# Routed experts: the second products' biases as one product with the masked gates

## The chip, the cores and the metric

One core of a Trainium2 chip. The metric is the time of one execution of the program on the device, in microseconds. The kernel before was timed in three runs: median 3362.38 us (3360.96 to 3362.39). The profiled execution took 3356.17 us by the same clock, and its span, from the first to the last recorded instruction, is 3354.4 us.

## What is computed

Two transformer blocks on 512 tokens of width 1024, one after the other, in float32. The change touches the last layer of the second block, a routed mixture of 32 experts: each token takes its four best experts, and their gates are the softmax of four router values. Cut to what matters:

```python
logits = (hf @ w_router + b_router).astype(jnp.float32)
top_val, top_idx = lax.top_k(logits, TOP_K)
gates = jax.nn.softmax(top_val, axis=-1)
...
def expert_block(args):
    e, tok, g = args
    xb = hf[tok]
    gu = xb @ w1[e] + b1[e]
    gate = jnp.minimum(gu[:, :D_FF], SWIGLU_LIMIT)
    up = jnp.clip(gu[:, D_FF:], -SWIGLU_LIMIT, SWIGLU_LIMIT)
    act = (up + 1.0) * gate * jax.nn.sigmoid(SWIGLU_ALPHA * gate)
    return (act @ w2[e] + b2[e]) * g[:, None]
...
out = jnp.zeros((n_tok, d), h.dtype).at[row_tok].add(y.reshape(n_rows, d))
```

`w1` is 1024 x 2048 per expert, `w2` 1024 x 1024, so each expert's weights are 12.6 MB. A token's row of the result is the sum over its experts of the gate times (`act @ w2[e] + b2[e]`); the part with the biases is, for all tokens at once, the matrix of the gates (512 x 32, zero where a token does not take an expert) times `b2` (32 x 1024).

## The kernel before, in words

A float32 product is made of three products of operands split into a high and a low part in the format fp32r: high x high, high x low, low x high (L1377 to L1379). For the weights ScalarE makes the high part (`wh`, L163) and VectorE, or for every twelfth piece GpSimd, the low part (`wl`, L164).

The experts run one after the other (`moe`, L1305 on). A block of 128 rows holds an expert's tokens; a loop at the end, for experts with more than 128 tokens, is not entered with these inputs. The weights come in pieces of 512 KB (256 input rows, 512 output columns), 24 per expert, into 17 raw buffers (`wr`) from SyncE's queue; a raw buffer is free again when its low part is made. `Feed` keeps up to five split pieces ahead of TensorE.

Per expert there are six products with 512 output columns: two for the gate half (`gate`), two for the up half (`up`), two for the second matrix (`outp`). Each (`product`, L1367) is 24 matmuls of 128 x 128 by 128 x 512 into one PSUM bank, and ahead of them one more (L1369) that puts the bias there: a column of `selr`, one-hot for the expert, times the tile `bias`, which holds the biases of all experts in rows 0 to 31 (high) and 32 to 63 (low). Four banks serve the products.

The gate half goes from PSUM through VectorE (`mg`, L1400), ScalarE (sigmoid `ms`, L1402) and VectorE (L1403); the up half through VectorE (`ms` L1409, `mact` L1410). `back` transposes `mact` on TensorE and splits it (`mah`, `mal`), `turn` does the same for the next expert's gathered rows `xf` (`mxh`, `mxl`), after ScalarE has scaled them (`scale`, L1388). `outp` evicts its two products on ScalarE into `my` (L1419), scaled by each row's gate. `my` is 128 x 1024 and has one buffer. `store` (L1422) is an indirect DMA from GpSimd's queue that adds the rows of `my` to the rows of `acc` in device memory; `begin` gathers rows of `hfd` in the same way (L1351).

Each engine works through its instructions in the order in which this code issues them. In iteration `e` of the main loop that is:

```python
n = begin(e + 1) if e + 1 < NE else None
b.up(0)
if prev:
    prev.store()
...
if n:
    n.scale()
b.gate(1, lambda: self.tokens(e + 2, g3(e + 2)) if e + 2 < NE else None)
```

and then `up(1)` with `back(0)` and the next expert's `turn` in its middle, the next expert's `gate(0)` with `back(1)` in its middle, and `outp`. `prev.store()` stands after `up(0)` of the next expert. `gates2` (L1229) runs once, after the first expert's `turn`: it normalises the gates (`gdn`, L1240) and cuts them into three bfloat16 parts (`g3`).

Of the kernel before, what the change touches and what calls it, by code (L numbers as in the profile page):

```python
# [7 lines left out]
F32 = mybir.dt.float32  # L8
F32R = mybir.dt.float32r
BF = mybir.dt.bfloat16  # L10
I32 = mybir.dt.int32
U32 = mybir.dt.uint32
AF = mybir.ActivationFunctionType
ALU = mybir.AluOpType
# [33 lines left out]
def layout(inp):  # L48
    f = lambda n: np.asarray(inp[n])
    pk = lambda w: w.reshape(-1, 128, w.shape[-1]).swapaxes(0, 1)  # L50
    chunk = lambda w, c: np.stack([pk(w[:, i:i + c]) for i in range(0, w.shape[1], c)])
    o = {}
    o["xT"] = pk(f("x")[0].T)
    o["pT"] = pk(f("p")[0, 0].T)
    o["memT"] = pk(f("mem_2")[0].T)
    o["w_in"] = chunk(f("w_in")[0][:, :1920], 128)
    o["w_in_v"] = pk(f("w_in")[0][:, 1920:])
    o["w_out"] = chunk(f("w_out")[0], 128)
    o["w_q"] = chunk(f("w_q")[0], 128)
    o["sk"] = f("sub_keys")[0].reshape(16, 128, 128).transpose(2, 0, 1)  # L60
    o["u_t"] = f("expert_u")[0].reshape(128, 128, 8, 128).transpose(0, 3, 2, 1)
    o["u_r"] = f("expert_u")[0]
    o["v_r"] = f("expert_v")[0]
    o["w_pe"] = chunk(f("w_pe")[0], 128)
    o["w_pg"] = chunk(f("w_pg")[0], 128)
    o["w_in_2"] = chunk(f("w_in_2")[0], 128)
    o["w_out_2"] = np.stack([chunk(f("w_out_2")[0][:512], 128), chunk(f("w_out_2")[0][512:], 128)])
    o["w_mem_q"] = chunk(f("w_mem_q_2")[0], 128)
    wide = lambda w: np.stack([np.stack([pk(w)[:, i:i + 2, j:j + 512] for i in range(0, 8, 2)]) for j in range(0, w.shape[1], 512)])
    o["w_mem_k"] = chunk(f("w_mem_kv_2")[0][:, :1024], 128)  # L70
    o["w_mem_v"] = wide(f("w_mem_kv_2")[0][:, 1024:])
    o["w_in_2v"] = wide(f("w_in_2")[0][:, 1024:1536])[0]
    o["w_mem_o"] = chunk(f("w_mem_o_2")[0], 128)
    o["w_pool"] = f("w_pool_2")[0].transpose(1, 0, 2)
    o["w_s"] = f("w_s")[0].transpose(2, 0, 1)
    o["w_router"] = pk(f("w_router_2")[0])
    o["w1"] = f("w_expert_in_2")[0].reshape(NE, 8 // CK, CK, 128, 4, 512).transpose(0, 4, 1, 3, 2, 5)
    o["w2"] = f("w_expert_out_2")[0].reshape(NE, 8 // CK, CK, 128, 2, 512).transpose(0, 4, 1, 3, 2, 5)
    b = np.concatenate([f("b_expert_in_2")[0], f("b_expert_out_2")[0]], 1)
    o["b12"] = np.concatenate([b, b, np.zeros((64, 3072), np.float32)], 0)  # L80
    cols = []
    for n in COLS:
        a = f(n)
        a = a.reshape(-1) if a.ndim == 1 else a[0]
        if n in ("conv_a_w", "conv_b_w"):
            cols.append(a.reshape(a.shape[0], -1, 128).transpose(2, 1, 0).reshape(128, -1))
        else:
            cols.append(a.reshape(-1, 128).T)
    o["cols"] = np.concatenate(cols, 1)
    row = lambda a: np.broadcast_to(a.reshape(1, -1), (128, a.size))  # L90
    o["rows"] = np.concatenate([row(f("ln_c_g")[0]), row(f("ln_c_b")[0]), row(f("b_router_2")[0]),
                                row(f("g_final_2")), row(f("g_ffn_2")[0])], 1)
    bs = f("b_s")[0].reshape(3, 2, 1, 128)
    o["b_s"] = np.broadcast_to(bs, (3, 2, 64, 128)).reshape(3, 128, 128).transpose(1, 0, 2)
    i = np.arange(128)
    one = np.float32(1)
    mats = [np.eye(128, dtype=np.float32), np.broadcast_to(i.astype(np.float32), (128, 128)),
            (i[:, None] < i[None, :]) * one, (i[:, None] >= i[None, :]) * one,
            (i[:, None] // 64 == i[None, :] // 64) * np.float32(1 / 64), np.ones((128, 128), np.float32)]
    sel = np.zeros((128, 128), np.float32)  # L100
    sel[:64, :32] = (i[:64, None] % 32 == i[None, :32])
    sel[:, 32] = i
    w = 2 ** (np.arange(4) + 1)
    t = np.arange(16)
    cnt = one / np.minimum(t[None, :] + 1, w[:, None]).astype(np.float32)
    sel[:, 64:128] = cnt.reshape(1, 64)
    mats.append(sel)
    o["consts"] = np.concatenate(mats, 1)
    return {k: np.ascontiguousarray(v) for k, v in o.items()}
# [37 lines left out]
class Body:  # L147
# [1085 lines left out]
    def gates2(self):  # L1233

        nc, cp, ge = self.nc, self.cp, self.ge
        sm = cp.tile([128, 4], F32, name="smm")
        nc.vector.tensor_reduce(sm, ge[:, :, 32:36], axis=AX.X, op=ALU.add)
        nc.vector.reciprocal(sm, sm)
        g = cp.tile([128, 4, 32], F32, name="gdn")
        nc.vector.tensor_tensor(g, ge[:, :, 0:32], sm.rearrange("p (t o) -> p t o", o=1).to_broadcast([128, 4, 32]), op=ALU.mult)  # L1240
        self.g3 = g3 = cp.tile([128, 4, 3, 32], BF, name="g3")
        for k in range(3):
            nc.vector.tensor_copy(g3[:, :, k], g)
            if k < 2:
                nc.vector.tensor_sub(g, g, g3[:, :, k])
# [59 lines left out]
    def moe(self):  # L1305
        tc, nc, A = self.tc, self.nc, self.A
        acc = self.acc
        hfd = self.hfd
        with ExitStack() as st:
            pool = lambda **k: st.enter_context(tc.tile_pool(bufs=1, **k))  # L1310
            xp = pool(name="xx")
            wst = st.enter_context(ExitStack())
            wp = wst.enter_context(tc.tile_pool(name="xw", bufs=1))
            rp = wst.enter_context(tc.tile_pool(name="xr", bufs=1))
# [1 line left out]
            bias = self.bias  # L1316
# [49 lines left out]

            def product(src, feed, sel, boff, mid=None):  # L1367
                ps = self.bank()
                nc.tensor.matmul(ps, sel.to_broadcast([128, 128]), bias[:, boff:boff + 512], start=True, stop=False)  # L1369
                for kk in range(8 // CK):  # L1370
                    if mid and kk == 4 // CK:
                        mid()
                    wh, wl = feed.take()
                    for k in range(CK):
                        i = CK * kk + k
                        a = src[0][:, i]
                        nc.tensor.matmul(ps, a, wh[:, k], start=False, stop=False)  # L1377
                        nc.tensor.matmul(ps, a, wl[:, k], start=False, stop=False)
                        nc.tensor.matmul(ps, src[1][:, i], wh[:, k], start=False, stop=(i == 7))  # L1379
                return ps  # L1380

            class Block:
# [32 lines left out]
                def outp(b, mid=None):  # L1415
                    b.y = y = xp.tile([128, 1024], F32, name="my", bufs=1)
                    for c in range(2):
                        ps = product(b.as_, b.feed, b.sel, 2048 + 512 * c, None if c else mid)
                        nc.scalar.activation(y[:, 512 * c:512 * c + 512], ps, AF.Copy, scale=b.f[:, 1:2])  # L1419

                def store(b):
                    nc.gpsimd.indirect_dma_start(out=acc, out_offset=bass.IndirectOffsetOnAxis(ap=b.ix, axis=0), in_=b.y,  # L1422
                                                 in_offset=None, bounds_check=511, oob_is_err=False, compute_op=ALU.add)

            def begin(e):
                return Block(xf, *self.xidx.pop(e), self.selr[:, e:e + 1], feed)
            g3 = lambda e: self.g3[:, :, :, e]
            b = begin(0)
# [14 lines left out]
            for e in range(NE):  # L1443
                n = begin(e + 1) if e + 1 < NE else None
                b.up(0)
                if prev:
                    prev.store()
                if e + 2 < NE:
                    self.places(e + 2)
                if e == 1:  # L1450
                    self.blocks()
# [4 lines that stand above are left out]
                def turns():  # L1456
                    b.back(0)
                    if n:
                        n.turn()
                b.up(1, turns)  # L1460
                if n:
                    n.gate(0, lambda: b.back(1))
                    b.outp()
                else:
                    b.outp(lambda: b.back(1))
                prev, b = b, n
# [5 lines left out]
            with tc.For_i(0, n, 1) as i:  # L1472
                j = nc.values_load(lst[0:1, bass.ds(i, 1)], engines=[mybir.EngineType.SP, mybir.EngineType.DVE],
                                   min_val=0, max_val=95)
                e = j % 32
# [14 lines left out]
                b = Block(xf, *self.xidx.pop("o"), s2, f2)  # L1490
# [12 lines left out]
            o = []  # L1503
# [39 lines left out]
```

## Time and profile before

| | before |
|---|---|
| median of 3 runs | 3362.38 us |
| profiled execution | 3356.17 us, span 3354.4 us |
| TensorE (PE) busy | 3139.9 us, 94% of the span |
| VectorE (DVE) busy | 2679.3 us, 80% |
| ScalarE (ACT) busy | 1756.8 us, 52% |
| GpSimd (POOL) busy | 1014.4 us, 30% |
| granted TensorE clock, mean | 0.974 |
| DMA | 819.30 MB, mean 244 GB/s |

The shares are means over stages of different kinds. The experts fill the span from about 2076 us to 3321 us, 1245 us for 32 experts. In the tables below, PE is TensorE's matmuls, PEld its weight loads, DVE VectorE, ACT ScalarE, POOL GpSimd and SP SyncE; times are in microseconds from the start of the span. The recorded end of a matmul is modelled and overlaps the next one, so of matmuls one reads the starts. In rows of the trace `L...` is a line of the kernel, `out<-in` are the program's names of tiles, and the brackets at the end hold the idle time of the engine before the instruction and what ended it.

### The profile page before, as it was taken

The page shows a single profiled execution, that of the slowest core. Times are in us where ns is not written, and L with a number is a line of the kernel's source. Part 1 is how long each engine was busy: PE and PEld are TensorE (multiplying, and loading weights), DVE is VectorE, ACT ScalarE, POOL GpSimd, SP SyncE. Part 2 cuts the span into 40 slices and gives each one's busy share as a digit, 9 for nine tenths or more (in the row PEclk, how much of TensorE's full clock was granted, in tenths as well). Part 3 has the DMA queues.
Part 4 walks back from the last instruction along what each step waited for, and adds up shares of the span by engine and source line. Part 5 has one row for each costly group of instructions (what it writes and reads, how often), then busy time and mean ns, then how long its engine had stood idle before and what let it go on. Part 6 is the DMA issues. An engine that isn't in the chain of part 4 may idle for free. (4 is left out here: it accounts for less than half of the span.)

```text
span 3354.4 us, 44364 instructions
## 1 busy us (share of the span) xinstructions
PE 3139.9 (94%) x15489; PEld 2645.6 (79%) x15489; DVE 2679.3 (80%) x4138; ACT 1756.8 (52%) x2297; POOL 1014.4 (30%) x617
## 2 busy tenths in 40 slices
PE   8999877999999999999999898999999999999995
PEld 6777776899999999998777665777777777777774
DVE  8968889677777777775756745999998999999995
ACT  4232366433333333333545433677777777777774
POOL 0004355344444444440444213222222222222221
PEclk9999888999999999999999998999999999999998
DMA  4342223788888988984211335899999999999994
GB/s 139 98 132 78 85 120 161 293 305 304 301 304 299 309 305 299 306 283 150 101 61 41 104 105 200 321 341 334 337 340 348 339 343 336 334 339 344 339 343 152
DMA packets 280244, 819.30 MB, mean 244 GB/s; under 512 B 29648, under 2 KB 91984, under 8 KB 278224
## 3 DMA queue, kind: packets, MB, share of 16 engines
q1 hardware_dynamic: 223760, 659.09, 55.2%
q0 software_dynamic: 46080, 151.04, 13.8%
q10 hardware_dynamic: 10176, 6.29, 0.6%
q8 instruction: 123, 2.02, 0.2%
q14 instruction: 105, 0.86, 0.1%
HBM read 782.74 MB, written 50.33 MB: 248 GB/s over the span
## 5 line engine op out<-in xcount | busy, mean ns | idle before, releaser
L180 PE MATMUL s<-nh,uh 128*128 128x384 f32 x1024 | 350.4, 342 | 9.7 <-ACT uh L163 9.6
L182 PE MATMUL s<-nh,ul 128*128 128x384 f32 x1024 | 349.2, 341 | 3.4 <-POOL ul L164 2.7
L181 PE MATMUL s<-nl,uh 128*128 128x384 f32 x1024 | 348.0, 340 | 0.0
L163 ACT ACTIVATE vh<-vr 128x1024 fp32r<-128x1024 f32 x128 | 135.9, 1062 | 311.3 <-issue 291.3
L555 POOL DMA_INDIRECT gr<-in_u_r_dram,ix x128 | 192.4, 1503 | 260.6 <-DVE dots L558 222.9
L555 POOL DMA_INDIRECT gr<-in_v_r_dram,ix x128 | 195.4, 1527 | 250.0 <-DVE o L561 218.4
L745 PE MATMUL a<-vh,gh 128*128 128x512 f32 x768 | 236.6, 389 | 0.0
L745 PE MATMUL a<-vl,gh 128*128 128x512 f32 x768 | 236.4, 389 | 0.0
L745 PE MATMUL a<-vh,gll 128*128 128x512 f32 x768 | 236.3, 389 | 0.0
L164 DVE TENSOR_TENSOR ul<-ur,uh 128x1024 fp32r<-128x1024 f32 x117 | 144.4, 1234 | 100.3 <-ACT uh L163 100.3
L164 DVE TENSOR_TENSOR vl<-vr,vh 128x1024 fp32r<-128x1024 f32 x128 | 156.6, 1224 | 67.7 <-ACT vh L163 67.7
L180 PEld LDWEIGHTS s<-nh,uh 128*128 128x128 f32 x1024 | 195.7, 191 | 14.7 <-ACT uh L163 10.5
L163 ACT ACTIVATE gh<-gl 128x384 fp32r<-128x384 f32 x128 | 67.3, 526 | 262.6 <-DVE gl L736 262.6
L182 PEld LDWEIGHTS s<-nh,ul 128*128 128x128 f32 x1024 | 195.0, 190 | 4.7 <-POOL ul L164 3.7
L181 PEld LDWEIGHTS s<-nl,uh 128*128 128x128 f32 x1024 | 195.2, 191 | 4.0
L163 ACT ACTIVATE uh<-ur 128x1024 fp32r<-128x1024 f32 x128 | 135.2, 1056 | 75.6 <-PE s L181 62.6
L745 PEld LDWEIGHTS a<-vl,gh 128*128 128x128 f32 x768 | 144.2, 188 | 30.2
L745 PEld LDWEIGHTS a<-vh,gll 128*128 128x128 f32 x768 | 144.2, 188 | 29.9
L561 DVE SCALAR_TENSOR_TENSOR o<-gr,dots,o 128x1024 f32<-128x1024 f32 x128 | 164.1, 1282 | 3.8 <-DMA gr<-in_v_r_dram,ix 1.2
L558 DVE CUSTOM_DVE_ANT_0 scr<-gr,n 128x1024 f32<-128x1024 f32 x128 | 156.4, 1222 | 4.8 <-DMA gr<-in_u_r_dram,ix 2.3
L727 PE MATMUL b<-ga,gb 128*128 128x128 f32 x768 | 118.8, 315 | 44.2 <-DVE gb L717 34.8
L745 PEld LDWEIGHTS a<-vh,gh 128*128 128x128 f32 x768 | 142.6, 188 | 21.4
(6594 smaller groups left out, 9342.5 us busy)
## 6 DMA issues: line engine op xcount, KB each, us to landing
wr<-in_w_dram SPq DMA_DIRECT2D x768, 512.0 KB, 6.1
ur<-in_u_t_dram SPq DMA_DIRECT2D x128, 512.0 KB, 5.0
vr<-in_v_r_dram SPq DMA_DIRECT2D x128, 512.0 KB, 6.7
gd<-stg SPq DMA_DIRECT2D x12, 2048.0 KB, 6.9
gt<-gd SPq DMA_DIRECT2D x32, 768.0 KB, 9.4
wqr<-in_w_q_dram SPq DMA_DIRECT2D x16, 512.0 KB, 3.6
wir<-in_w_in_dram SPq DMA_DIRECT2D x15, 512.0 KB, 3.6
wlr<-in_w_in_dram SPq DMA_DIRECT2D x12, 512.0 KB, 3.7
```

What stands on the lines that cost most here:

```text
L163: self.nc.scalar.activation(hi, raw, AF.Copy)
L164: (eng or self.nc.vector).tensor_sub(lo, raw, hi.bitcast(F32))
L180: mm(ps, ah, bh, start=(k == 0 and start), stop=False)
L181: mm(ps, ah, bl, start=False, stop=False)
L182: mm(ps, al, bh, start=False, stop=(k == n - 1 and stop))
L555: nc.gpsimd.indirect_dma_start(out=r, out_offset=None, in_=src, in_offset=bass.IndirectOffsetOnAxis(ap=ix3[:, i:i + 1], axis=0))
L558: nc.vector.tensor_tensor_reduce(scr, r, n3, op0=ALU.mult, op1=ALU.add, scale=1.0, scalar=0.0, accum_out=dots[:, i:i + 1])
L561: nc.vector.scalar_tensor_tensor(o3, r, dots[:, i:i + 1], o3, op0=ALU.mult, op1=ALU.add)
L727: nc.tensor.matmul(ps[:, 128 * i:128 * i + 128], bb[:, i], a[:, i], start=True, stop=True)
L745: mm(acc[t][c], a[:, ts], v[:, 512 * c:512 * c + 512], start=(e == 0 and a is gh and v is vh), stop=(e == 127 and a is gl))
```

## The change

The second matrix's bias leaves the `outp` products: `product` takes `None` for the column of `selr`, and the first of the 24 matmuls then opens the bank. That takes out two L1369 matmuls per expert, 64 in all. In their place the masked gates are transposed once in `gates2`, into a tile `gT` of 96 rows (the gates' high part twice, and their low part), and `bias` gets a third copy of the biases in rows 64 to 95. `biased(t)` multiplies 128 tokens' columns of `gT` with the biases, two matmuls of 128 x 512, evicts them on ScalarE into `my`, and adds them to the tokens' rows of `acc` by another accumulating DMA. It is called for `t` = 0 to 3 in the iterations `e` = 3 to 6, right behind `prev.store()`.

```diff
-    o["b12"] = np.concatenate([b, b, np.zeros((64, 3072), np.float32)], 0)
+    o["b12"] = np.concatenate([b, b, b, np.zeros((32, 3072), np.float32)], 0)
...
         self.g3 = g3 = cp.tile([128, 4, 3, 32], BF, name="g3")
+
+        pt = self.bank("x")
+        gc = self.xp.tile([128, 512], F32, name="mg", bufs=2)[:, 0:384].rearrange("p (t k e) -> p t k e", t=4, k=3)
+        for k in range(3):
+            nc.vector.tensor_mul(gc[:, :, k], g, self.M)
+        for t in range(4):
+            nc.tensor.transpose(pt[0:96, 128 * t:128 * t + 128], gc[:, t].rearrange("p k e -> p (k e)"), self.ident)
+        self.gT = self.xp.tile([96, 512], F32R, name="gT")
+        nc.scalar.activation(self.gT, pt[0:96], AF.Copy)
+        nc.vector.tensor_sub(self.gT[64:96], pt[64:96], self.gT[64:96].bitcast(F32))
+        self.row = self.xp.tile([128, 4], I32, name="row")
+        for t in range(4):
+            nc.vector.tensor_scalar_add(self.row[:, t:t + 1], self.pcol, 128.0 * t)
...
-                nc.tensor.matmul(ps, sel.to_broadcast([128, 128]), bias[:, boff:boff + 512], start=True, stop=False)
+                if sel is not None:
+                    nc.tensor.matmul(ps, sel.to_broadcast([128, 128]), bias[:, boff:boff + 512], start=True, stop=False)
...
-                        nc.tensor.matmul(ps, a, wh[:, k], start=False, stop=False)
+                        nc.tensor.matmul(ps, a, wh[:, k], start=(sel is None and i == 0), stop=False)
...
-                        ps = product(b.as_, b.feed, b.sel, 2048 + 512 * c, None if c else mid)
+                        ps = product(b.as_, b.feed, None, 0, None if c else mid)
...
+            def biased(t):
+
+                y = xp.tile([128, 1024], F32, name="my", bufs=1)
+                for c in range(2):
+                    ps = self.bank()
+                    nc.tensor.matmul(ps, self.gT[:, 128 * t:128 * t + 128], bias[0:96, 2048 + 512 * c:2560 + 512 * c],
+                                     start=True, stop=True)
+                    nc.scalar.activation(y[:, 512 * c:512 * c + 512], ps, AF.Copy)
+                nc.gpsimd.indirect_dma_start(out=acc, out_offset=bass.IndirectOffsetOnAxis(ap=self.row[:, t:t + 1], axis=0),
+                                             in_=y, in_offset=None, bounds_check=511, oob_is_err=False, compute_op=ALU.add)
...
                 if prev:
                     prev.store()
+                if 3 <= e < 7:
+                    biased(e - 3)
```

ScalarE's order in iteration `e` = 3, before, from the second eviction of the last expert's `outp` on (L163: high parts of weights; L1388: scaling of the gathered rows; L1402: the gate's sigmoid; in brackets the counters that an instruction waits for, DMAHW those of plain loads, DMASW those of GpSimd's DMAs):

```order
L1419 ACTIVATE my<-b,fx 128x512 [waits PE_49]
L163 ACTIVATE wh__18322<-wr_16517 128x1024 [waits DMAHW4_49,DVE_49]
...
L163 ACTIVATE wh__18355<-wr_17086 128x1024 [waits DMAHW7_49,DVE_49]
L1388 ACTIVATE xf<-xf,fx 128x1024 [waits DMASW6_49]
L163 ACTIVATE wh__18380<-wr_17087 128x1024 [waits DMAHW0_49,DVE_49,PE_49]
```

And with the change, where L1433, L1402 and L1446 are the eviction of `outp`, the scaling and the eviction in `biased`:

```order
L1433 ACTIVATE my<-b,fx 128x512 [waits PE_49]
L163 ACTIVATE wh__18333<-wr_16517 128x1024 [waits DMAHW4_49,DVE_49]
...
L163 ACTIVATE wh__18366<-wr_17086 128x1024 [waits DMAHW7_49,DVE_49]
L1446 ACTIVATE my<-b 128x512 [waits DMASW7_49,PE_49,Activation_49]
L1446 ACTIVATE my<-b 128x512 [waits PE_49]
L1402 ACTIVATE xf<-xf,fx 128x1024 [waits DMASW6_49]
L163 ACTIVATE wh__18401<-wr_17087 128x1024 [waits DMAHW0_49,DVE_49]
```

Two evictions now stand between the four splits and the scaling, and the first waits for a DMA of GpSimd. GpSimd's order at the same place, with the change (L1436: `store`; L1447: the store in `biased`; L1364: the gather):

```order
L164 TENSOR_TENSOR wl__18367<-wr_17086,wh__18366 128x1024 [waits PE_49,DMAHW7_49,Activation_49,Pool_49]
L1436 DMA acc<-my,ix 512x1024 [waits DMASW5_49]
L1447 DMA acc<-my,row 512x1024 [waits DMASW7_49,DMASW0_49,Activation_49]
L164 TENSOR_TENSOR wl__18585<-wr_16509,wh__18584 128x1024 [waits DVE_49,PE_49,DMAHW3_49,Activation_49,Pool_49]
L1364 DMA xf<-hfd,ix 128x1024 [waits DMASW1_49]
```

The split and the store stand as before, and a second store that waits for the counter of the first (DMASW7) follows. TensorE's order at the start of the experts, with the change (L1372: transposes of the gathered rows; L1248: transposes of the masked gates; L1383: the bias of the first `gate` product):

```order
L1372 MATMUL x<-consts,xf 128x128 x7
L1248 MATMUL x<-consts,mg 96x128 [waits DMAHW4_49,DMAHW5_49,DMAHW2_49,DMAHW6_49,DMAHW1_49,DMAHW7_49,DMAHW0_49,DVE_49]
L1248 MATMUL x<-consts,mg 96x128 x3
L1383 MATMUL b<-bias,selr 128x512
```

Before, the bias of the first product followed the transposes of `xf` directly; now four transposes that wait for VectorE stand between them.

## Rows read from the trace of the kernel before

**Rows 1.** Table of stretches: length, busy time per engine, granted clock, DMA share, GB/s.

```profile
2200.00:2300.00 100.00, 97.42 (x470) 78.35 (x469) 90.39 (x105) 73.42 (x86) 22.27 (x10) 1.00 0.95 348
...
3000.00:3200.00 200.00, 192.42 (x916) 154.40 (x915) 182.62 (x208) 146.04 (x170) 44.36 (x21) 1.00 0.93 336
...
2245.00:2250.00 5.00, 5.00 (x23) 4.04 (x22) 3.67 (x4) 5.00 (x6) 1.38 (x1) 1.00 1.02 418
```

**Rows 2.** Waits, 2100 to 3315 us: total us, times, longest; PE, then DVE.

```profile
PE x L1359 <- DVE mact L1410: 37.1, 32, 1.7
...
DVE ms L1409 <- PE b L1379: 20.8, 31, 0.7
...
DVE wl__18680 L164 <- ACT wh__18679 L163: 1.0, 1, 1.0
```

**Rows 3.** Timeline of TensorE in one expert: start, duration, instruction.

```profile
2249.63 0.40 PE L1369 MATMUL b<-bias,selr 128*128 128x512 f32 x1
...
2256.53 0.40 PE L1378 MATMUL b<-wl__18738,mxh 128*128 128x512 f32 x1
...
2267.58 0.63 PE L1359 MATMUL x<-consts,mact 128*128 128x128 f32 x4 [1.20 <-DVE mact L1410]
...
2270.84 0.40 PE L1369 MATMUL b<-bias,selr 128*128 128x512 f32 x1
...
2276.66 0.39 PE L1369 MATMUL b<-bias,selr 128*128 128x512 f32 x1
```

**Rows 4.** Timeline of VectorE in the same expert.

```profile
2252.68 1.22 DVE L164 TENSOR_TENSOR wl__18738<-wr,wh__18737 128x1024 fp32r<-128x1024 f32 x1
...
2258.73 0.69 DVE L1403 TENSOR_TENSOR mg<-mg,ms 128x512 f32<-128x512 f32 x1 [0.70 <-ACT ms L1402]
...
2266.74 0.69 DVE L1410 SCALAR_TENSOR_TENSOR mact<-ms,mg 128x512 f32<-128x512 f32 x1
```

**Rows 5.** Timeline of ScalarE in the same expert.

```profile
2248.37 1.14 ACT L1388 ACTIVATE xf<-xf,fx 128x1024 f32<-128x1024 f32 x1
2249.41 1.05 ACT L163 ACTIVATE wh__18737<-wr 128x1024 fp32r<-128x1024 f32 x1
...
2276.86 0.69 ACT L1419 ACTIVATE my<-b,fx 128x512 f32<-128x512 f32 x1 [0.30 <-PE b L1379]
```

**Rows 6.** Timeline of GpSimd in the same expert.

```profile
2248.62 2.80 POOL L164 TENSOR_TENSOR wl__18713<-wr,wh__18712 128x1024 fp32r<-128x1024 f32 x1 [12.14 <-ACT wh__18712 L163]
2251.58 1.85 POOL L1422 DMA_INDIRECT acc<-my,ix  x1 [0.16 <-issue]
2270.88 2.82 POOL L164 TENSOR_TENSOR wl__18921<-wr,wh__18920 128x1024 fp32r<-128x1024 f32 x1 [17.44 <-ACT wh__18920 L163]
```

**Rows 7.** Tile `acc`, stores at 2212.89 and 2290.28; chain of waits, last store.

```profile
DMA to landing us min/median/max: 9.1/9.1/9.1
...
DMA to landing us min/median/max: 7.2/7.2/7.2
...
3321.55 6.08 DMA acc<-my,ix
```

**Rows 8.** Timeline of TensorE in the first expert.

```profile
2094.50 0.79 PE L1287 MATMUL x<-tok,ohe 128*128 128x4 bf16 x8 [1.43 <-DVE ohe L1276]
...
2095.26 0.77 PE L1377 MATMUL b<-wh__17254,mxh 128*128 128x512 f32 x1
...
2098.40 0.48 PE L1378 MATMUL b<-wl__17266,mxh 128*128 128x512 f32 x1
```

**Rows 9.** Timelines of TensorE and VectorE at the experts' start.

```profile
2074.80 1.97 PE L1359 MATMUL x<-consts,xf 128*128 128x128 f32 x8 [6.56 <-ACT xf L1388]
2076.42 0.78 PE L1369 MATMUL b<-bias,selr 128*128 128x512 f32 x1
...
2078.44 0.29 DVE L1240 TENSOR_TENSOR gdn<-ge,smm 128x128 f32<-128x128 f32 x1
2078.77 0.23 DVE L1243 CAST g<-gdn 128x128 bf16<-128x128 f32 x1
```

More of the change, by code (lines that the diff above doesn't have):

```diff
@@ L1310, in moe @@
             pool = lambda **k: st.enter_context(tc.tile_pool(bufs=1, **k))
-            xp = pool(name="xx")
+            xp = self.xp = pool(name="xx")
             wst = st.enter_context(ExitStack())
```

## The prediction

> **What bounds the kernel now.** I read the table of stretches first [rows 1]. From 2100 us to 3315 us the kernel is in the 32 experts of the second block, and there TensorE is busy 97% of the time at a granted clock of 1.00 (the upper of its two levels, 2.4 GHz), VectorE 90 to 91%, ScalarE 73%, the DMA engines 93 to 95%. So the reader is to see a stage in which three resources stand close together; which of them ends last has to be read from the waits. In the list of waits of that stage [rows 2] TensorE waits for one thing that matters: the transposes of `mact` wait for VectorE, 32 times, 37.1 us in all. VectorE waits 31 times for the end of the first `up` product (20.8 us), and once per expert 1.0 us for a half split by ScalarE. No engine waits for a weight load.
>
> The timeline of one expert shows how this closes to a loop [rows 3, 4]. TensorE finishes the first `up` product at about 2249.63, VectorE takes it up, and from `wl__18738` at 2252.68 it works in its fixed order, without a gap other than the 0.70 us inside the gate, up to `mact` at 2266.74. TensorE waits 1.20 us for that, and starts the transposes at 2267.58. From there on TensorE has no wait until that product, and VectorE has some slack. So an expert has **one half set by VectorE's queue (2249.6 to 2267.6) and one half set by TensorE (2267.6 to the next first `up` product)**. What is saved on TensorE counts if it lies in the second half. What is late for VectorE counts if it lies in the first.
>
> **The sum, part by part**, against the profiled execution (3356.17 us, span 3354.4); the median of the runs shown, 3362.38, is 6.2 us above it, and I add the difference to the median.
>
> *Bias products taken out.* Each expert loses the two first matmuls of its `outp` products, 64 in all. From one of them to the next there are 25 matmuls in 2276.66 − 2270.84 = 5.82 us [rows 3], so 0.233 us each. Both lie in the half that TensorE sets. 64 × 0.233 = **−14.9 us**. VectorE's slack there (1.0 and 0.67 us per expert [rows 2]) covers 0.47 us, and the DMA engines move 418 GB/s in a short stretch [rows 1] against a mean of 336 to 348, so they can follow.
> The Trainium skill ("TensorE: Matmul & The Clock Gate", section "Back-to-back issue gap") gives 131 ns for a 512-column matmul in a sustained stream of weight loads and matmuls; by that the 64 would be worth 8.4 us. The rows above say 233 ns, and they decide.
>
> *Bias products put in.* Eight matmuls of the same form, two in each of four experts, 8 × 0.233 = 1.9 us, between the first `up` and the second `gate` product. TensorE is going to wait there anyway (next part), so I take 0; if that cover were gone, +1.9.
>
> *The write of `my` in `biased`.* This is where the change costs. `my` has one buffer. `prev.store()` hands it to the accumulating DMA, and the very next thing ScalarE is asked for is to overwrite it. In the order above ScalarE's first L1446 waits for that DMA's semaphore, and behind it on ScalarE stand the scaling of `xf` and the splits of the weights that TensorE needs next. In the trace of before ScalarE gets to this place at 2248.37 (it started the scaling of `xf` there) [rows 5]. The store cannot have begun by then: GpSimd first does its share of the splits, 2248.62 to 2251.42, and starts the store at 2251.58 [rows 6]. From start to landing the store takes between 9.1 and 7.2 us in these four experts (the first is the longest, the third the shortest), and 6.1 in the last store of the program, with nothing beside it [rows 7]. Since ScalarE's stop also stops the freeing of weight buffers, the queue of loads runs dry while it waits, so I take 7.2, with 6.1 and 9.1 as ends. Then ScalarE goes on at 2251.58 + 7.2 = 2258.8. Two evictions of 0.69, the scaling of 1.14 and the split `wh__18737` of 1.05, each starting 0.1 before the one ahead ends [rows 5], end 3.3 us later, at 2262.1. VectorE started `wl__18738` at 2252.68, so it is 9.4 us late, and by rows 4 it cannot make that up before `mact`. It delays TensorE's transposes by the same amount. 4 × 9.4 = **+37.6 us** (ends 4 × 8.3 = 33.2 and 4 × 11.3 = 45.2).
> TensorE itself misses `wl__18738` from 2256.53 on [rows 3]: it would be ready 1.2 us after 2262.1, so TensorE is 6.8 us late by its own need. That is less than 9.4, which is why I count VectorE's lateness.
> The second half of a wait: the biased store on GpSimd waits for the store before it and for ScalarE. It starts near 2260.3 and lands some 7 us later; the next writer of `my` comes at 2276.86 + 9.4 [rows 5], so nothing waits for it. GpSimd's next split comes at 2270.88 [rows 6], also later.
>
> *The clock.* At 2094.50 TensorE had waited 1.43 us and then had only short matmuls; the seven after that start 0.43 us and more apart, the lower level (1.2 GHz), and cost 3.14 − 7 × 0.233 = 1.5 us [rows 8]. The first slow stretch in each of the four experts comes behind the 6.8 us and is hidden by the 9.4. Then TensorE waits again, for `mact`, by 1.2 + 9.4 − 6.8 − 1.5 = 2.3 us; the waits of 1.2 us left the granted clock at 1.00 [rows 1]. I take a second slow stretch in two of four cases: **+3.0 us** (ends 0 and 6.0).
>
> *The start.* `gates2` runs once. TensorE's first product started at 2076.42; now four transposes stand before it that wait for three multiplications behind `gdn` (2078.44) [rows 9]. Three multiplications of 0.29 us end near 2079.6, four transposes by the row of eight in 1.97 us (0.2 apart) end near 2080.4; ScalarE evicts and VectorE subtracts in 0.69 each, by the eviction of rows 5, and VectorE makes four one-column indices (I estimate 0.5 us in all), so its own work goes on at about 2082.3 instead of 2078.77. VectorE is 3.5 us late, TensorE 4.0, and nothing covers it: **+3.7 us** (ends 3.5 and 4.6, the latter with some matmuls behind the longer wait at the lower clock).
>
> Sum: −14.9 + 37.6 + 3.0 + 3.7 = +29.4 us. 3362.4 + 29.4 = **3391.8, I say 3391 us** (0.9% slower). With the ends it runs from −14.9 + 33.2 + 3.5 = +21.8 (3384) to −14.9 + 45.2 + 6.0 + 4.6 = +40.9 (3403).
>
> **The rivals.**
> *TensorE's own need decides.* If VectorE, once the splits come, can take later work earlier than rows 4 let me think, only the 6.8 us per expert count: −14.9 + 27.2 + 3.7 = +16, 3378 us. Against it: VectorE's gapless order from 2252.68 to 2266.74.
> *The store lands much sooner once the loads stop.* ScalarE stands still, the DMA engines are free, and the wait shrinks. The quiet row (6.1) bounds it at 8.3 us per expert. If the landing took 3.2 us, VectorE would be 5.4 us late: −14.9 + 21.6 + 3.7 = +10, 3373 us.
> The Trainium skill ("DMA: Bandwidth & Descriptors", section "Anatomy of one DMA — SWDGE (gpsimd) path") fits 2.0 us plus the bytes over 436 GB/s per DMA, an estimate of 3.2 us for these 512 KB; the accumulating stores of this trace take 6.1 at the least, so it speaks against that rule here.
> *The write does not wait (faster).* ScalarE's stop is harmless if the eviction of the bias finds `my` free: then the change is worth −14.9 + 3.7 = −11.2, 3351 us. The place is the single buffer of `my`, and it decides at 2.8 us of lateness per expert (11.2 / 4). That would need a landing 0.6 us after the store's start. Only the order's semaphore being an earlier DMA's could give it.
> *The gain is not paid out.* If the weight loads (0.93 to 0.95 of the DMA engines) hold the experts at their present pace, the −14.9 is lost: +44, 3407 us. Against it: no wait for a load in the list.
>
> **How the numbers follow.** About 0.2% (6.7 us) is what a measurement of this kernel can tell from no change. Chances: the forecast 0.74, TensorE's own need 0.10, the quick landing 0.06, the write that does not wait 0.05, the lost gain 0.05. The range of 8 in 10 takes the forecast's own 3384 to 3403 and reaches down over the two milder slow cases: 3372 to 3404. Faster by over 0.2%: 0.05; within: 0.03, for a mild case milder than worked out; slower: 0.92.
>
> **What the profile of the changed kernel would show.** Right: in four experts ScalarE's first L1446 waits about 10 us for the DMA `acc<-my`, 32 product starts of `outp` come without a bias row, the `mact` transposes of these four experts come 9 to 10 us later than in their neighbours, and an expert outside them takes 0.47 us less. Wrong: if ScalarE's wait is under 3 us, or if the four experts are longer by 5 us or less, or if the neighbours are no shorter than before.

## The result and the profile after

The changed kernel takes 3394.11 us (median of six runs, 3386.3 to 3396.47), the kernel before, timed beside it, 3362.39 us (six runs, 3360.1 to 3363.55). The ratio is 1.0092, with a 95% interval of 1.0079 to 1.0105: slower by 31.7 us. Forecast were 3391 us, 3372 to 3404, with a chance of 0.92 for slower. The profiled execution of the changed kernel took 3393.86 us, its span 3392.1 us, at a mean granted clock of 0.969.

The waits of the changed kernel, 2100 to 3360 us, in the columns of [rows 2] (line numbers are the changed kernel's: L1446 is the eviction in `biased`, L1447 its store, L1436 `prev.store()`, L1391 to L1393 the three products, L1424 the old L1410):

```profile
ACT my L1446 <- DMA acc<-my,ix: 46.9, 4, 12.5
PE x L1372 <- DVE mact L1424: 38.7, 32, 1.7
POOL acc L1447 <- ACT my L1446: 32.5, 4, 9.0
DVE ms L1423 <- PE b L1393: 21.1, 31, 0.7
...
DVE wl__18767 L164 <- ACT wh__18766 L163: 11.2, 1, 11.2
DVE wl__18402 L164 <- ACT wh__18401 L163: 10.8, 1, 10.8
...
PE b L1391 <- ACT wh__18766 L163: 7.4, 1, 7.4
PE b L1391 <- ACT wh__18401 L163: 7.0, 1, 7.0
```

The first row was not there before: ScalarE stands four times, 11.7 us each, until the store of the last expert has landed. The wait passes on to VectorE (10.8 and 11.2 us in the first two of the four experts, 9.2 and 10.2 in the others, 41.4 in all) and to TensorE (7.0 and 7.4; 5.4 and 6.4). The wait for `mact`, the largest of TensorE's before, stays what it was.

What that costs is read from GpSimd's timeline, since `prev.store()` stands once in every expert, at the same place (L1436):

```profile
2183.05 1.87 POOL L1436 DMA_INDIRECT acc<-my,ix  x1 [0.16 <-issue]
2221.36 1.84 POOL L1436 DMA_INDIRECT acc<-my,ix  x1 [0.17 <-issue]
2231.77 1.55 POOL L1447 DMA_INDIRECT acc<-my,row  x1 [8.56 <-ACT my L1446]
2270.73 1.84 POOL L1436 DMA_INDIRECT acc<-my,ix  x1 [0.16 <-issue]
...
2320.48 1.84 POOL L1436 DMA_INDIRECT acc<-my,ix  x1 [0.16 <-issue]
...
2368.30 1.84 POOL L1436 DMA_INDIRECT acc<-my,ix  x1 [0.16 <-issue]
...
2417.04 1.86 POOL L1436 DMA_INDIRECT acc<-my,ix  x1
```

From one L1436 to the next an expert outside the four takes 38.31 us (2183.05 to 2221.36); before it was 38.70 (2251.58 to 2290.28 [rows 6, 7]). The four with a biased store take 49.37, 49.75, 47.82 and 48.74 us, so 42.4 us more than four times 38.31, or 10.6 us each.

ScalarE's timeline in the changed kernel, for the first of the four and the next two waits, shows the chain behind it [rows 5 for the same place before]:

```profile
2217.20 1.05 ACT L163 ACTIVATE wh__18366<-wr 128x1024 fp32r<-128x1024 f32 x1
2230.41 1.09 ACT L1446 ACTIVATE my<-b 128x512 f32<-128x512 f32 x2 [12.16 <-DMA acc<-my,ix]
2231.38 1.15 ACT L1402 ACTIVATE xf<-xf,fx 128x1024 f32<-128x1024 f32 x1
2232.42 1.05 ACT L163 ACTIVATE wh__18401<-wr 128x1024 fp32r<-128x1024 f32 x1
...
2280.18 1.08 ACT L1446 ACTIVATE my<-b 128x512 f32<-128x512 f32 x2 [12.55 <-DMA acc<-my,ix]
...
2327.99 1.08 ACT L1446 ACTIVATE my<-b 128x512 f32<-128x512 f32 x2 [10.61 <-DMA acc<-my,ix]
```

The store that starts at 2221.36 lets ScalarE go on at 2230.41, 9.05 us later; the next three take 9.45, 7.51 and 8.43 (the last from 2368.30 to an eviction at 2376.73). Their mean is 8.6 us, some 0.15 us of it behind the landings that the profile gives for these stores (8.9, 9.3, 7.4 and 8.3). VectorE and TensorE in the same expert, by their timelines:

```profile
2233.51 1.23 DVE L164 TENSOR_TENSOR wl__18402<-wr,wh__18401 128x1024 fp32r<-128x1024 f32 x1 [10.77 <-ACT wh__18401 L163]
...
2239.58 0.69 DVE L1417 TENSOR_TENSOR mg<-mg,ms 128x512 f32<-128x512 f32 x1 [0.70 <-ACT ms L1416]
...
2247.59 0.69 DVE L1424 SCALAR_TENSOR_TENSOR mact<-ms,mg 128x512 f32<-128x512 f32 x1
```

```profile
2219.41 0.63 PE L1444 MATMUL b<-bias,gT 96*128 96x512 f32 x2
...
2226.15 0.39 PE L1383 MATMUL b<-bias,selr 128*128 128x512 f32 x1
2233.53 0.80 PE L1391 MATMUL b<-wh__18401,mxh 128*128 128x512 f32 x1 [6.99 <-ACT wh__18401 L163]
...
2235.81 0.63 PE L1391 MATMUL b<-wh__18401,mxh 128*128 128x512 f32 x1
2236.24 0.63 PE L1392 MATMUL b<-wl__18402,mxh 128*128 128x512 f32 x1
...
2248.43 0.63 PE L1372 MATMUL x<-consts,mact 128*128 128x128 f32 x4 [1.68 <-DVE mact L1424]
```

From its first split to `mact` VectorE needs 2247.59 − 2233.51 = 14.08 us; before, 2266.74 − 2252.68 = 14.06 [rows 4]. It made up nothing. TensorE waits 6.99 us, then its matmuls start 0.43 us apart, and at the end it still waits 1.68 us for `mact`. The table of stretches shows the clock of that piece, and how the DMA engines go on and then stop (columns as in [rows 1]):

```profile
2221.00:2226.00 5.00, 5.00 (x33) 3.89 (x33) 1.74 (x5) 0.00 (x0) 2.04 (x2) 1.00 1.03 398
2226.00:2231.00 5.00, 0.54 (x3) 0.11 (x1) 0.00 (x0) 0.59 (x2) 0.00 (x0) 1.00 0.34 75
2231.00:2236.00 5.00, 2.01 (x4) 1.31 (x5) 2.49 (x5) 5.00 (x7) 1.55 (x1) 0.54 0.46 60
2236.00:2241.00 5.00, 5.00 (x25) 4.18 (x24) 4.04 (x6) 2.40 (x4) 0.00 (x0) 0.77 0.97 320
2241.00:2256.00 15.00, 13.17 (x58) 10.11 (x57) 14.21 (x16) 11.20 (x15) 4.13 (x2) 1.00 0.86 295
```

Granted clock 0.54 and 0.77 behind the long wait, that is, a piece at the lower level (1.2 GHz), then 1.00, also over the wait for `mact` at 2248. In the other three experts the 15 us with that wait show 1.00 as well.

The DMA engines did not stop with ScalarE. They were full for the first 4.6 us of the store (1.03, 398 GB/s), and only then ran dry. The view of the DMA queues shows whose packets moved (q1: SyncE's loads; q0: GpSimd's queue, here this store; packets, MB, share of 16 engines), from 2221.4 to 2224.8 and from there to 2230.4:

```profile
q1 hardware_dynamic: 386, 1.40, 102.9%
...
q0 software_dynamic: 144, 0.35, 32.0%
q1 hardware_dynamic: 136, 0.46, 21.0%
```

For 3.4 us only loads moved; the store's own packets came behind them. The biased store that follows, at 2231.77, finds the DMA engines idle: its first packets come 2.0 us behind its start. The DMA issues between 2100 and 2400 us, with their median landing, set the two kinds side by side:

```profile
acc<-my,ix POOLq DMA_INDIRECT x6, 8.7
acc<-my,row POOLq DMA_INDIRECT x4, 5.9
```

The four biased stores landed in 5.8 to 6.0 us, although each moves more (0.52 MB against the 0.35 of the store at 2221.36).

At the start of the experts TensorE, in the same timeline, now waits for the masked gates [rows 9]:

```profile
2081.08 1.97 PE L1372 MATMUL x<-consts,xf 128*128 128x128 f32 x8 [6.19 <-ACT xf L1402]
2085.80 1.09 PE L1248 MATMUL x<-consts,mg 128*96 128x128 f32 x4 [2.75 <-DVE mg L1246]
2086.54 0.78 PE L1383 MATMUL b<-bias,selr 128*128 128x512 f32 x1
```

The first product starts 5.46 us behind the first transpose of `xf`, before it was 1.62. From the router's matmuls to the first `prev.store()` the changed kernel takes 69.69 us and the kernel before 67.10, so 2.6 us of that were not covered.

The two profiled executions differ by 37.7 us. Of that 6.7 us lie ahead of the experts, in stages that the change doesn't touch (the router's matmuls start at 2072.39, before at 2065.73; in the runs below they start between 2062.69 and 2072.50, whatever was changed). The rest: 2.6 at the start, 30.8 from the first to the last `prev.store()` (the 42.4 less some 12 for the shorter experts), −2.3 behind the last.

### The profile page after: what moved, and what is told of

It is laid out like the page before. It is cut to its first block, busy times and chain, and to the rows that moved or that the text cites. A ratio compares the mean times of both kernels' runs of the same rounds, so it can differ in the third digit from the quotient of the medians.

```text
span 3392.1 us, 44298 instructions
## 1 busy us (share of the span) xinstructions
PE 3146.9 (93%) x15437; PEld 2644.8 (78%) x15437; DVE 2680.7 (79%) x4146; ACT 1760.5 (52%) x2306; POOL 1021.6 (30%) x621
## 5 line engine op out<-in xcount | busy, mean ns | idle before, releaser
L163 ACT ACTIVATE vh<-vr 128x1024 fp32r<-128x1024 f32 x128 | 135.9, 1061 | 312.3 <-issue 292.2
L163 ACT ACTIVATE gh<-gl 128x384 fp32r<-128x384 f32 x128 | 67.2, 525 | 261.6 <-DVE gl L736 261.6
L163 ACT ACTIVATE uh<-ur 128x1024 fp32r<-128x1024 f32 x128 | 135.2, 1056 | 75.6 <-PE s L181 62.7
```

The source lines that it names most:

```text
L163: self.nc.scalar.activation(hi, raw, AF.Copy)
```

## The experiments

The theory: the change costs its 42 us because ScalarE overwrites `my` while the store just issued still reads it, and everything behind that write on ScalarE is late; the product itself costs nothing, and the matmuls taken out bring what they should. Rivals: the second store or its traffic; the added matmuls and evictions; the start; for the size, TensorE's own wait (5.4 to 7.4 us) instead of VectorE's (9.2 to 11.2). Each run is compared with runs of the kernel before on the same chip: 3359.53 us for the first four experiments, 3360.29 us for the last three. The ratios are those on record; the quotient of two medians differs from them by up to 0.0007.

**A tile of its own (e1_own_buffer).** Same place, same stores, but another tile; to make room, one raw weight buffer less.

```diff
-NRAW, NRAW2 = 14, 3
+NRAW, NRAW2 = 14, 2
-                y = xp.tile([128, 1024], F32, name="my", bufs=1)
+                y = xp.tile([128, 1024], F32, name="mb", bufs=1)
```

> The bias product's rows get a buffer of their own (mb); to make room there are 16 raw weight buffers in place of 17. Theory (the four long experts are ScalarE's wait for the store that reads my, and nothing else of the added work): ScalarE's L1446 no longer waits for a DMA, the four iterations are as long as their neighbours (38.3 to 39 us from store to store), and the time is the one before less 0.38 us in each of 32 experts plus about 3 us at the start: -9 us, 3353, ratio 0.997. Rival (the added work itself is dear: eight matmuls, eight evictions and four more accumulating DMAs on busy queues): the four iterations stay several us longer, and the time stays above the one before, 3365 to 3390. Rival to the side: one raw buffer fewer starves the splits: every iteration gets longer, not only four.

Measured: 3350.51 us, ratio 0.9968 (0.9956 to 0.998). ScalarE's only wait at this line, in the list of this kernel, is for the product itself:

```profile
ACT mb L1446 <- PE b L1444: 6.4, 4, 1.6
```

The four experts take 38.81 us, half a microsecond more than their neighbours (38.31). So the second store, its traffic, the evictions and the fewer raw buffers cost next to nothing; the wait for the buffer was the cost. The 0.5 us look like the two matmuls (2 × 0.233), but VectorE's timeline shows another cause. Its first split in one of the four experts, and in the first expert behind them:

```profile
2223.21 1.23 DVE L164 TENSOR_TENSOR wl__18399<-wr,wh__18398 128x1024 fp32r<-128x1024 f32 x1 [0.20 <-ACT wh__18398 L163]
...
2377.97 1.21 DVE L164 TENSOR_TENSOR wl__19849<-wr,wh__19848 128x1024 fp32r<-128x1024 f32 x1
```

VectorE took up the first `up` product at 2219.88 and at 2375.11, so the split comes 3.33 us behind that in the one and 2.86 in the other. ScalarE's 1.6 us of waiting for the product and its two evictions put the high part off, and VectorE passes 0.47 of that on; up to the `mact` that TensorE waits for, the lateness is 0.49 (17.41 against 16.92 us). TensorE's wait there gets longer, not shorter (1.36 us against 1.2), so the two matmuls themselves are covered.

**No biased product at all (e2_no_biased).**

```diff
-                if 3 <= e < 7:
-                    biased(e - 3)
```

> The calls of biased are left out: the second products' biases are in no output, the gates are still masked and transposed. Theory: as in e1, 3353 (-9 us): the gain of the 64 matmuls less the start; e1 and e2 within 2 us of each other. Rival (the added work is dear beside the wait): e2 is faster than e1 by 5 us or more.

Measured: 3348.45 us, 0.9967 (0.9954 to 0.998), every expert but the first and the last two 38.30 to 38.34 us. The intervals of this and the last run overlap: the 2 us between them can't be told apart in time, only in the traces (4 × 0.5 us).

**Only the gates' preparation (e3_gates_only).** The kernel before, with the new lines of `gates2`, and nothing that uses them; the biases stay in the `outp` products.

> The kernel before plus the masking and transposing of the gates at the start alone; the result is used by nothing, the biases stay in the second products. Theory: only the start costs, TensorE's first expert product comes about 3 to 4 us later against the router's matmuls: +3 to +4 us, 3366, ratio 1.001. Rival (the start is covered, or it throws the order of the first experts out): 0, or +6 and more. If the longer matmul spacing seen with the change (0.234 against 0.233 us in the experts) comes from the new tiles' places in memory, it shows here too, as some 0.15 us per expert, +5 us more.

Measured: 3366.19 us, 1.0014 (1.0004 to 1.0024). The start takes 70.17 us from the router's matmuls to the first store (67.10 before): +3.1. And every expert takes 38.77 us instead of 38.70, though the loop issues the same instructions. The timeline of TensorE shows it in the `outp` products, 25 matmuls from one row to the next:

```profile
2280.93 0.39 PE L1383 MATMUL b<-bias,selr 128*128 128x512 f32 x1
2286.78 0.39 PE L1383 MATMUL b<-bias,selr 128*128 128x512 f32 x1
```

That is 5.85 us, before 5.82 [rows 3]: each matmul starts 0.234 us behind the last instead of 0.233. All eight traces with the new lines have this spacing (0.2340 to 0.2341 us in the mean of over 2600 intervals each, before 0.2328). What these lines can change for the loop is where things lie in memory; that this is the cause is argued from that alone and was not tried. Against this kernel the experts of the changed one save 38.77 − 38.31 = 0.46 us, two matmuls of 0.23.

**A later place (e4_later_place).** Same single buffer, but called behind the second `up` product, where the store has long landed.

```diff
-                if 3 <= e < 7:
-                    biased(e - 3)
...
                 b.up(1, turns)
+                if 3 <= e < 7:
+                    biased(e - 3)
                 if n:
                     n.gate(0, lambda: b.back(1))
```

> The change as it is, one buffer for my, but biased is called after the second up product of the same iteration, some 13 us later, where the store that reads my should have landed. Theory: ScalarE's first L1446 waits for no DMA or under 1 us, and the time is near that of e1: 3353 to 3357 (the two matmuls now lie in the half that VectorE sets, and the two evictions delay ScalarE by 1.2 us in four experts). Rival (an expert with two accumulating stores is slow wherever the second stands): several us per such expert, 3370 and more.

Measured: 3349.20 us, 0.9962 (0.995 to 0.9975). ScalarE's timeline has no wait at the line at all:

```profile
2232.68 1.09 ACT L1446 ACTIVATE my<-b 128x512 f32<-128x512 f32 x2
```

All experts but the first and the last two take 38.29 to 38.34 us. With the whole change in it this kernel is faster than the one before and than the changed one. The two matmuls now stand ahead of TensorE's wait for `mact`, and that wait gets shorter by as much, 0.68 us instead of 1.2:

```profile
2236.43 0.63 PE L1372 MATMUL x<-consts,mact 128*128 128x128 f32 x4 [0.68 <-DVE mact L1424]
```

This run also holds the biased store with the loads still beside it. Of the one that starts at 2310.68 no packet moves up to 2314.2; all 144 move between 2314.2 and 2320.2, the last of them over 9 us behind its start:

```profile
q0 software_dynamic: 144, 0.52, 58.7%
```

In the changed kernel the same store (2329.34), with idle DMA engines, has landed after 5.9 us.

**Eight waits with half the value each (e5_eight_waits).** The original place and buffer, iterations 3 to 10.

```diff
-                if 3 <= e < 7:
-                    biased(e - 3)
+                if 3 <= e < 11:
+                    biased((e - 3) % 4)
...
-                    nc.scalar.activation(y[:, 512 * c:512 * c + 512], ps, AF.Copy)
+                    nc.scalar.activation(y[:, 512 * c:512 * c + 512], ps, AF.Copy, scale=0.5)
```

> The biased product is made in eight iterations (3 to 10) at the place of the change, each time with half the value, so every token's biases are added in two halves. Theory (each call costs a fixed lateness: the store's landing plus what stands behind it on ScalarE): the eight iterations are each 10 to 11 us longer than their neighbours (the change's four: 47.82 to 49.75 against 38.31, mean 10.6), so about 4 x 10.6 = 42 us over the change, near 3436 us. Rival (the four iterations are costly because of something that happens once, a disturbance from which the feed of weights has to recover, and which would be shared by calls in a row): less than 30 us over the change, and the later calls cheaper than the first four.

Measured: 3435.94 us, 1.022 (1.0206 to 1.0234), 41.8 us over the changed kernel's median.

```profile
ACT my L1446 <- DMA acc<-my,ix: 93.8, 8, 12.6
```

In the list of waits it is again 11.7 us each, and the eight experts take 48.15 to 49.78 us, 85.0 us more than eight times 38.31: 10.6 each, as with four. The cost goes by the wait.

**In the middle of the second gate product (e7_middle).** Same buffer and wait, but ScalarE has the scaling of the rows and two more splits done when it comes to it.

```diff
-                if 3 <= e < 7:
-                    biased(e - 3)
...
-                b.gate(1, lambda: self.tokens(e + 2, g3(e + 2)) if e + 2 < NE else None)
+                def mid():
+                    if e + 2 < NE:
+                        self.tokens(e + 2, g3(e + 2))
+                    if 3 <= e < 7:
+                        biased(e - 3)
+                b.gate(1, mid)
```

> Same single buffer, same wait, but the call stands in the middle of the second gate product (behind the tokens of expert e + 2), so that ScalarE has the scaling of the gathered rows and two more splits behind it when it comes to the wait. Theory (what counts is how late VectorE gets the first split behind the wait): the landing of the store ends at the same time, some 8.6 us after the store's start, but VectorE has two splits' work (2 x 1.23 us and what stands between them) before it runs dry, and the scaling (1.1 us) is no longer between the wait and the next split; so the lateness falls from 10.6 us per call to some 6.5 to 7.5, 4 x 7 = 28 us over the 38.31 of the neighbours, near 3377 us. Rival (the disturbance is the store's or the loads' own, wherever ScalarE stands): the four iterations stay near 48 to 50 us, 3392 us. Rival (TensorE's own need decides): 4 x 3 = 12 us or less, 3362 us or below.

Measured: 3381.32 us, 1.0059 (1.0046 to 1.0073). The four experts take 46.19, 46.15, 46.10 and 45.39 us, 7.6 more than their neighbours each; a tenth over the 7 of the expectation; the stores land 8.5 to 9.3 us after their start here instead of 8.6. The waits between 2200 and 2400 us:

```profile
ACT my L1446 <- DMA acc<-my,ix: 37.0, 4, 9.5
...
DVE wl__18806 L164 <- ACT wh__18805 L163: 7.8, 1, 7.8
...
PE b L1391 <- ACT wh__18805 L163: 1.9, 1, 1.9
```

This tells VectorE and TensorE apart. TensorE's own wait for the first split is 1.9 us here, VectorE's is 7.8, and the expert is late by VectorE's. Over the four experts VectorE's waits are 30.3 us, TensorE's 6.7, and the experts are late by 30.6.

**The preparation off the start (e6_off_start).** The later place, and the masking, transposing and splitting of the gates in iteration 2 (`masked` and `turned` hold the lines taken out of `gates2`).

```diff
...
                 if n:
+                    if e == 2:
+                        self.masked()
+                    def mid0():
+                        b.back(1)
+                        if e == 2:
+                            self.turned()
-                    n.gate(0, lambda: b.back(1))
+                    n.gate(0, mid0)
```

> The later place of e4_later_place, and besides the masking and transposing of the gates is moved from the start of the experts into iteration 2: the three multiplications behind up(1), the four transposes, the eviction, the subtraction and the four index columns into the middle of the next expert's gate(0), where TensorE sets the pace; the residual of the gates' three parts gets a place of its own so that the gates survive. Theory: the start is back to the 67.1 us between the router's matmuls and the first store (70.1 in e3_gates_only and e4_later_place), iteration 2 pays about 0.8 us for four transposes and whatever of VectorE's 2 us its slack does not hold, so 2 to 3 us below e4_later_place: 3346 to 3347 us, ratio to before about 0.9955. Rival (the start's 3 us were not these instructions but another placement of tiles): the start stays near 70 us and the time near 3349.

Measured: 3350.68 us (ten runs, 3342.13 to 3355.24), 0.9975 (0.9964 to 0.9985): not to be told from the later place alone. In the trace the start is back at 66.26 us, as the theory has it, but iteration 2 takes 40.80 us instead of 38.31, so 2.5 us and not the 0.8 to be paid for. VectorE's timeline there, at the four index columns and the split behind them:

```profile
2192.55 0.34 DVE L1267 TENSOR_SCALAR row<-consts 128x1 int32<-128x1 f32 x4
2192.80 3.07 DVE L164 TENSOR_TENSOR wl__18210<-wr,wh__18209 128x1024 fp32r<-128x1024 f32 x1
```

The split takes 3.07 us where its neighbours take 1.22, just while GpSimd makes a split of its own (2192.39 to 2194.79). TensorE then waits for `wl__18210` and `wl__18239`. The kernel before has the like in every expert. Its `mact`, issued at 2250.55 while GpSimd's split runs (2248.62 to 2251.42 [rows 6]), takes twice the 0.69 us that it takes without one [rows 4]:

```profile
2250.55 1.42 DVE L1410 SCALAR_TENSOR_TENSOR mact<-ms,mg 128x512 f32<-128x512 f32 x1
```

Both end behind GpSimd's split, by 1.08 and 0.55 us, nearly the time that each takes alone. So the place chosen for the preparation pushed VectorE's split under GpSimd's; that it is this that costs the 2.5 us was not tried by itself, and moving the preparation brought nothing that can be measured.

## Why the prediction was right

| term | predicted | shown | by |
|---|---|---|---|
| bias matmuls out | −14.9 | −12 | 31 intervals × 0.39 |
| matmuls put in | 0 | 0 | covered by the wait; in e4 by the wait for `mact` |
| the write of `my` | +37.6 | +42.4 | four experts over their neighbours |
| clock, second piece | +3.0 | 0 | granted clock 1.00 at `mact` |
| start | +3.7 | +2.6 to 3.1 | first store behind the router; e3 |
| sum | +29.4 | +33 | medians: +31.7 |

*The write of `my`: right in mechanism, low in size.* ScalarE's wait, its releaser and its place are as forecast, and taking away what it waits for, in two ways (e1, e4), takes away the whole cost. The mis-sized term is the store's landing. I took 7.2 us, the shortest of the four before [rows 7], "since ScalarE's stop also stops the freeing of weight buffers, the queue of loads runs dry". The queue did run dry, but too late for this store: the loads that were already on their way filled the DMA engines for 4.6 of its 9.05 us, and it met them as the stores of before had. The landings of the four experts were 9.1, 8.6, 7.2 and 7.9 us before and 8.9, 9.3, 7.4 and 8.3 with the change. The dry queue helped only the biased stores, which nothing waits for (5.8 to 6.0 us, where I had some 7). With 8.6 instead of 7.2 the step gives 10.8 per expert, and 10.6 were measured.
The Trainium skill ("DMA: Bandwidth & Descriptors", section "Anatomy of one DMA — SWDGE (gpsimd) path") would give 3.2 us, an estimate from its fit for 512 KB; neither the 7.4 to 9.3 us beside loads nor the 5.8 to 6.0 us of the biased stores, which started with idle DMA engines, agree with it.

*Which engine's lateness counts: right.* TensorE's own waits for the first split sum to 26.2 us in the changed kernel, and with four waits of 0.5 for `wl` behind them are 28.2, close to the 27.2 of that rival. But the experts are late by 42.4, VectorE's waits sum to 41.4, and e7 pulls the two apart (6.7 against 30.3).

*The matmuls taken out: right, a fifth too large.* The half of the expert that TensorE sets passes the gain on; no load or VectorE took it back. The step that failed is "64 × 0.233": it assumed that all other matmuls stay as they are, and they moved apart by half a per cent, which e3 shows without the change in the products; why they did stays open.
The Trainium skill ("TensorE: Matmul & The Clock Gate", section "Back-to-back issue gap") has 131 ns for a 512-column matmul in a sustained stream of weight loads and matmuls, which makes an estimate of 0.26 us for the two of an expert; the 0.46 between e3 and the changed kernel do not agree with it.

*The clock: wrong, and small.* The piece at the lower level behind the long wait came and was hidden under VectorE's lateness, as forecast. The second one, "in two of four cases", did not come: the waits for `mact` were 6.2 us in four, and the clock stayed at 1.00.

*The start: right, at the low side.* TensorE's first product is 3.84 us later against the transposes (forecast 4.0), and about one of these was made up by the first store.

The errors of the terms offset each other in part: +4.8 for the landing, +3 for the gain, −3 for the clock, −1 for the start. That the forecast of 3391 us came within some 3 us of the median is partly luck.

Of the rivals, the quick landing fell with the 7.51 to 9.45 us until ScalarE went on, the write that does not wait with the 46.9 us of waits, the lost gain with the 38.31 us per expert, TensorE's own need with e7.

## What to carry to other kernels

Look at what the engine that reuses a buffer has queued behind it. Here ScalarE, which works in order, overwrote a tile whose store was issued only after it had got there, and stopped until that store had landed (11.7 us). The price was not its own wait but how late the next engine got what stood behind (10.6 us). The same product, evictions and store, put where the landing is over (e4) or into a tile of their own (e1), turned 0.9% slower into some 0.3 to 0.4% faster. For the price take the landing from the middle or the top of the range that the trace shows for stores that start in the same traffic. Ask when the wait will empty the DMA engines: here they stayed full for the first half of the landing, so the store that caused the stop gained nothing by it.

## What was not expected

The store that stopped ScalarE did not land sooner for the stop: 9.05 us from 2221.36 on, with the DMA engines full up to 2226 and at 0.34 and 75 GB/s behind that. The stores that started once they were idle did, in 5.8 to 6.0 us, like the last store of the program with nothing beside it (6.02 to 6.08). By these rows a store's landing goes by what the DMA engines still have to do when it starts.

The distance of equal matmuls depends on something outside the loop: 5.82 us for 25 of them before, 5.85 with the gates' preparation and its tiles ahead of the experts, which is 0.07 us per expert or 2.2 us in all, about a seventh of what the matmuls taken out were to bring.
